# An opening of a two-layer diffusion backbone with its conditioning in four chunks of two feature tiles

## The chip, the cores and the metric

The kernel runs on one core of one Trainium2 chip. The metric is the device time of one execution in microseconds (us). The kernel before takes 2668.5 us, the median of three runs (2668.33 to 2669.18).

## What is computed

A backbone of two layers over 512 latent tokens and 256 context tokens with 1024 features. At the head of each layer stands a conditioned norm: two conditioning vectors (c for the latent tokens, c_ctx for the context) are multiplied with a 1024 x 6144 matrix, and the first two blocks of 1024 columns of the result are the shift and the scale of the first norm. Only layer 0's first norm, its conditioning and the first products behind it bear on this change.

```python
silu_c, silu_cc = jax.nn.silu(c), jax.nn.silu(c_ctx)
for l in range(DEPTH):
    mod_lat = (silu_c @ ada_w[l] + ada_b[l])[:, None, :]
    mod_ctx = silu_cc @ ada_w[l] + ada_b[l]
    sh1, sc1, g1, sh2, sc2, g2 = jnp.split(mod_lat, 6, axis=-1)
    csh1, csc1, cg1, csh2, csc2, cg2 = jnp.split(mod_ctx, 6, axis=-1)
    h_lat = modulate(rmsnorm(x, norm1_g[l]), sh1, sc1)      # h * (1 + scale) + shift
    h_ctx = modulate(rmsnorm(ctx, norm1_g[l]), csh1, csc1)
    z_lat = h_lat @ w_in[l]
    z_ctx = h_ctx @ w_in[l]
    ...
```

Behind it come attention, two other branches and a feed-forward network, which the change leaves as they are. Everything is fp32.

## The kernel before

**Layout.** Activations lie feature-major: eight tiles x of 128 features by 768 tokens (T); `pa` is the part of the 512 latent tokens, `pb` that of the 256 context tokens, and index s (0 latent, 1 context) picks the modulation `mod[0][s]` (in listings mod00 and mod01). The norm's output of tile k is held as two tiles, `hh` (rounded to fp32r, TensorE's fast fp32 format) and `hl` (what the rounding left).

**Products.** A gemm (L164 to L186) takes each product of two fp32 matrices as three of fp32r ones: whi x hh (L183), whi x hl (L184), wlo x hh (L186). `Stream` brings the weights in halves of 512 KB on SP's DMA queue (L62) into two raw buffers; ACT casts whi (L83), and VectorE subtracts wlo (L69). With `late` set, wlo is written where `low()` stands and not at once. The products of silu(c) with the conditioning matrix are plain fp32 ones instead ("whole" here): stationary `silu` (128 x 2), moving 512 columns (L216).

**The opening**, `startup` (L413). SP's queue brings the eight x tiles (384 KB each) with the raw conditioning tiles (512 KB each, `Raw`, L113, seven buffers) between them. The conditioning of shift and scale goes in chunks n of 512 columns, each of four raw tiles: n=2 is the scale of tiles 0 to 3, n=0 their shift; n=3 and n=1 are scale and shift of tiles 4 to 7. `ada_pe` makes a chunk's eight products on TensorE, copies the sum from PSUM (L222, ACT), turns it with four small products against `ident` (L228) and adds the bias (L206). n=2 and n=0 are made this way while x arrives. Beside them `sq_acc` squares each x (ACT, L317 and L323) and sums the squares (VectorE, L324), `norm_stat` brings the sum across features with small products (L335) and takes the inverse root on VectorE, and `norm_rows` spreads it over the partitions (TensorE L349, ACT copy L351, tile rb).

**The norm and the first gemm.** `scales_set` (L308) makes acol = (1 + scale) * g. `norm_apply` (L360) makes for each tile nt = x * acol * rb (VectorE, L367), hh = nt + shift (ACT, L376) and hl = nt + shift - hh (VectorE, L379). The gemm that eats them is that of three weight halves (keys "c"); `step(k, part, i)` issues the three products of tile k, token part and half i. Tiles 0 to 3 come first, latent then context; in between go chunk n=3 on VectorE (`ada_dve`: sixteen multiply-adds of 512 columns, L244 and L246, then small products against `ones`) and chunk n=1 on TensorE, two products at a time. Then follow tiles 4 to 7, and `finish(pb, 4)` issues the context part of tiles 4 to 7 half by half and evacuates each half (`c_first`: ACT copies halves 0 and 2, L792; VectorE multiplies half 1 into the copy of half 0, L794). Then `attn_load` sends two transfers (rl and cs, 256 KB each) from POOL's queue (L594, L596), and the query/key products of layer 0 (L647) begin.

**What sets the order.** Nothing reorders: each engine works through its own list in program order, which the Python code above writes out by hand. A tile of a rotating buffer (`bufs=2`) waits until the last reader of the one before it is done; a DMA on SP's queue that waits for its buffer holds the DMAs behind it.

## Time and profile before

| what | us |
|---|---|
| median of three runs | 2668.5 |
| the profiled execution's own time | 2669.8 |
| its span (first to last instruction) | 2667.9 |
| TensorE busy in the span | 2613.4 (98%) |
| VectorE, ACT, POOL busy | 1630.2, 1035.4, 220.3 |
| mean granted clock of TensorE over the span | 0.995 |

The page of the profile comes from one execution. "Granted clock" is the TensorE clock that the throttle gave, as a share of full speed. A busy TensorE is not one at its peak: its products overlap, and their ends are modelled, so the opening is read by the starts of its products. Times are from the span's start.

### The profile page before, as it was taken

What the parts mean: (1) busy time and instruction counts of PE and PEld (TensorE: products, weight loads), DVE (VectorE), ACT (ScalarE), POOL (GpSimd) and SP (SyncE); (2) the same over time, 40 slices, a digit from 0 to 9 for tenths busy, and PEclk for the clock granted to TensorE, in tenths of its full rate; (3) what the DMA queues carried; (4) which work ended last, traced back from release to release, by engine and by line L of the source; (5) the groups of instructions that cost most, each with busy time, mean ns of one, the idle gap of its engine ahead of it and who ended that gap; (6) DMA issues with size and microseconds to landing.
All of it is one profiled execution on the core that took longest, in us unless ns stands there. A gap on an engine that the chain in (4) does not pass through costs nothing.

```text
span 2667.9 us, 37365 instructions
## 1 busy us (share of the span) xinstructions
PE 2613.4 (98%) x15128; PEld 2265.6 (85%) x15128; DVE 1630.2 (61%) x2887; ACT 1035.4 (39%) x1840; POOL 220.3 (8%) x202
## 2 busy tenths in 40 slices
PE   7999999999999999999999999999999999999999
PEld 3899999888888888888888878898988888888887
DVE  5677777656546537544544577777767554654544
ACT  3455555542122224312312344555563232443422
POOL 0000000001111110100100100000001122010101
PEclk9999999999999999999999999999999999999999
DMA  5211211224333332222222231212124545233233
GB/s 225 82 44 58 63 67 44 65 67 148 105 125 111 103 127 66 78 86 73 79 79 79 91 108 60 68 53 63 56 72 170 174 165 182 72 100 100 93 103 111
DMA packets 79660, 254.36 MB, mean 95 GB/s; under 512 B 9200, under 2 KB 19712, under 8 KB 79104
## 3 DMA queue, kind: packets, MB, share of 16 engines
q1 hardware_dynamic: 64512, 196.64, 22.7%
q0 software_dynamic: 14544, 55.07, 6.3%
q8 instruction: 119, 1.95, 0.3%
q14 instruction: 53, 0.43, 0.0%
q10 hardware_dynamic: 432, 0.27, 0.0%
HBM read 234.63 MB, written 6.82 MB: 91 GB/s over the span
## 4 chain that ended last, share of the span: by engine, by line
PE 82%; DVE 10%; ACT 4%; DMA 2%; issue 1%; SPq 0%; POOL 0%; ACTq 0%; POOLq 0%; DVEq 0%
PE mm L183 22%; PE mm L186 22%; PE mm L184 22%; PE S L857 3%; DVE wlo L69 2%; PE mm L647 2%; PE mm L649 2%; PE mm L648 2%; ACT whi L83 1%; PE mmT L893 1%; DMA qT<-qT 1%; ACT pa L869 1%; DVE zs L697 1%; DVE al L898 1%; PE mmT L906 1%
## 5 line engine op out<-in xcount | busy, mean ns | idle before, releaser
L183 PE MATMUL mm<-hh,whi 128*128 128x512 f32 (+1 forms) x2392 | 853.3, 357 | 7.3 <-ACT hh L376 5.5
L184 PE MATMUL mm<-hl,whi 128*128 128x512 f32 (+1 forms) x2392 | 818.8, 353 | 6.9 <-DVE hl L379 6.5
L186 PE MATMUL mm<-hh,wlo 128*128 128x512 f32 (+1 forms) x2392 | 751.3, 353 | 1.3 <-DVE wlo L69 1.3
L183 PEld LDWEIGHTS mm<-hh,whi 128*128 128x128 f32 x2392 | 451.8, 189 | 99.9 <-ACT hh L376 9.3
L69 DVE TENSOR_TENSOR wlo<-wraw,whi 128x1024 fp32r<-128x1024 f32 x320 | 399.0, 1247 | 196.6 <-ACT whi L83 194.8
L184 PEld LDWEIGHTS mm<-hl,whi 128*128 128x128 f32 x2392 | 452.1, 189 | 72.2 <-DVE hl L379 13.7
L186 PEld LDWEIGHTS mm<-hh,wlo 128*128 128x128 f32 x2392 | 414.0, 190 | 40.7 <-DVE wlo L69 3.0
L83 ACT CAST whi<-wraw 128x1024 fp32r<-128x1024 f32 x320 | 334.9, 1048 | 284.0 <-PE mm L184 243.2
L1018 DVE SCALAR_TENSOR_TENSOR cv<-mm,pc,cv 128x511 f32<-128x511 f32 (+1 forms) x132 | 86.8, 657 | 181.4 <-ACT cv L1017 180.5
L869 ACT ACTIVATE pa<-S,mn 128x768 f32<-128x768 f32 (+1 forms) x160 | 129.3, 813 | 154.7 <-DVE mn L864 127.3
L183 PE MATMUL mm<-ah,whi 128*128 128x512 f32 (+1 forms) x528 | 187.9, 356 | 0.0
L647 PE MATMUL mm<-whi,hh 128*128 128x256 f32 x640 | 183.5, 287 | 1.3 <-DVE cp L794 0.8
L648 PE MATMUL mm<-wlo,hh 128*128 128x256 f32 x640 | 181.1, 283 | 0.0
L649 PE MATMUL mm<-whi,hl 128*128 128x256 f32 x640 | 181.1, 283 | 0.0
L184 PE MATMUL mm<-al,whi 128*128 128x512 f32 (+1 forms) x528 | 179.9, 354 | 0.0
L186 PE MATMUL mm<-ah,wlo 128*128 128x512 f32 (+1 forms) x528 | 161.7, 355 | 0.0
L1017 ACT ACTIVATE cv<-mm,pc 128x512 f32<-128x512 f32 (+1 forms) x132 | 88.7, 705 | 176.9 <-PE mm L186 176.9
L1179 DVE SCALAR_TENSOR_TENSOR x<-mm,mod,x 128x512 f32<-128x512 f32 (+1 forms) x91 | 58.2, 659 | 139.0 <-PE mm L186 139.0
L1222 POOL TENSOR_TENSOR cv<-cv 128x768 f32<-128x768 f32 (+1 forms) x44 | 91.5, 2080 | 601.2 <-DVE cv L1020 419.9
L857 PE MATMUL S<-kT,qT 128*128 128x512 f32 x576 | 119.1, 343 | 11.4 <-DMA qT<-qT 9.7
L647 PEld LDWEIGHTS mm<-whi,hh 128*128 128x128 f32 x640 | 122.5, 191 | 4.3 <-ACT cp L792 1.0
L864 DVE TENSOR_REDUCE mn<-S 128x1 f32<-128x768 f32 x128 | 116.2, 948 | 12.8 <-PE S L857 12.8
(237 smaller groups left out, 4035.2 us busy)
## 6 DMA issues: line engine op xcount, KB each, us to landing
wraw<-w SPq DMA_DIRECT2D x320, 512.0 KB, 3.6
araw<-ada POOLq DMA_DIRECT2D x80, 512.0 KB, 4.0
qT<-qT SPq DMA_DIRECT2D x80, 128.0 KB, 3.9
araw<-ada SPq DMA_DIRECT2D x16, 512.0 KB, 8.7
x<-xT SPq DMA_DIRECT2D x8, 384.0 KB, 7.4
srow<-sscr POOLq DMA_DIRECT2D x3, 1024.0 KB, 6.1
x<-xT POOLq DMA_DIRECT2D x8, 384.0 KB, 6.4
xscr<-x SPq DMA_DIRECT2D x8, 256.0 KB, 4.0
```

The source lines that it names most:

```text
L69: self.lo_eng.tensor_tensor(lo, raw, hi.bitcast(F32), ALU.subtract)
L83: self.nc.scalar.copy(hi, raw)
L183: nc.tensor.matmul(ps[:, :m], lhsT=hh, rhs=xh[:, o:o + m], start=st, stop=False)
L184: nc.tensor.matmul(ps[:, :m], lhsT=hh, rhs=xl[:, o:o + m], start=False, stop=False)
L186: nc.tensor.matmul(ps[:, :m], lhsT=hl, rhs=xh[:, o:o + m], start=False, stop=sp)
L647: nc.tensor.matmul(ps[:, :256], lhsT=hh[:, sl], rhs=hi[:, c:c + 256], start=(k == 0), stop=False)
L648: nc.tensor.matmul(ps[:, :256], lhsT=hh[:, sl], rhs=lo[:, c:c + 256], start=False, stop=False)
L649: nc.tensor.matmul(ps[:, :256], lhsT=hl[:, sl], rhs=hi[:, c:c + 256], start=False, stop=(k == 7))
L857: nc.tensor.matmul(s[:, c0 + o:c0 + o + m], lhsT=st["q"][:, v, a, t0:t0 + 128], rhs=st["k"][a][:, k0 + o:k0 + o + m], start=(v == 0), stop ...
L864: nc.vector.tensor_reduce(mn[:, a:a + 1], ss[a], AX.X, ALU.min)
L869: nc.scalar.activation(pa[:, :nk], ss[a], AF.Exp, bias=mn[:, a:a + 1], scale=-1.0, accum_out=sm[a])
L1222: nc.gpsimd.tensor_tensor(cs[1][:, :n], cs[1][:, :n], cs[0][:, :n], ALU.mult)
```

## The change

`startup` is written anew. The conditioning is cut into four chunks j, each of two feature tiles (2j and 2j+1) with both shift and scale: 256 columns of the one and 256 of the other, in four raw tiles of 512 KB as before. The host packs the matrix so (`layout`).

- Chunks 0 and 1 are whole fp32 products as before (`ada_pe` with `whole`, eight each).
- Chunks 2 and 3 are split: `ada_split` casts a raw tile to ahi on ACT (L213) and subtracts alo (L215) on VectorE for the even pieces, on POOL for the odd ones; ahi and alo have two buffers each. The stationary side, `silu4`, has four columns (hi and lo of the two vectors), and TensorE makes 16 fp32r products of 512 moving columns for each such chunk (L229). `sel4` adds hi and lo in the four small products that turn a chunk's sum (L240).
- `ada_dve` is gone. The raw conditioning tiles have five buffers and not seven. The squares of an x tile are taken over its 768 columns at once.
- `norm_apply` makes the tiles in pairs, since each pair waits for its chunk's scale (`cut`). rb and the context's nt lie in other buffers. `finish(pb, 6)` is left with two tiles for each half, and the steps of the three halves, the pieces of the chunks and the pairs of tiles are interleaved in a new written order.

Line numbers of the changed kernel: nt L354, hh L363, hl L366, statistics L322, row spread L336, chunk's products L229, its copy L236, its small products L240.

The core of the diff. Functions that are new or written anew stand in full, every line marked +; their old text stands above:

```diff
+    def ada_split(self, l, j, i):
+        nc = self.nc
+        raw = self.ast.take("s", l, j, i)
+        hi = self.ast.pool.tile([128, 1024], F32R, tag="ahi", bufs=2, name="ahi")
+        nc.scalar.copy(hi, raw)
+        lo = self.ast.pool.tile([128, 1024], F32R, tag="alo", bufs=2, name="alo")
+        (nc.vector, nc.gpsimd)[i % 2].tensor_tensor(lo, raw, hi.bitcast(F32), ALU.subtract)
+        self.ast.load_to(len(self.ast.keys) + self.ast.bufs)
+        self.parted.append((hi, lo))
...
+    def ada_pe(self, l, j, ps, whole):
+        nc = self.nc
+        nr = 2 if whole else 4
+        for i in range(4):
+            if whole:
+                parts = [self.ast.take("s", l, j, i)]
+            else:
+                parts = self.parted.pop(0)
+            for q in (0, 1):
+                for p, w in enumerate(parts):
+                    nc.tensor.matmul(ps[0:nr, :], lhsT=(self.silu if whole else self.silu4)[:, 2 * i + q, :],
+                                     rhs=w[:, q * 512:q * 512 + 512], start=(i == q == p == 0),
+                                     stop=(i == 3 and q == 1 and p == len(parts) - 1))
+            if whole:
+                self.ast.load_to(len(self.ast.keys) + self.ast.bufs)
+            yield
+        rows = self.small.tile([4, 512], F32, tag="adarow", bufs=1, name="adarow")
+        nc.scalar.copy(rows[0:nr], ps[0:nr, :])
+        yield
+        pt = self.ad.tile([128, 512], F32, tag="ad", name="ad")
+        for i in range(4):
+            nc.tensor.matmul(pt[:, 2 * i:2 * i + 2], lhsT=rows[0:nr, i * 128:(i + 1) * 128], rhs=self.sel4[0:nr, :],
+                             start=True, stop=True)
+        pv = pt[:, 0:8].rearrange("p (t k s) -> p s t k", t=2, s=2)
+        cut = lambda a: a.rearrange("p (t k) -> p t k", t=2)[:, :, 2 * j:2 * j + 2]
+        for s in range(2):
+            nc.vector.tensor_tensor(cut(self.mod[l][s][:, 0:16]), pv[:, s], cut(self.pc[l][:, PC_ADAB:PC_ADAB + 16]), ALU.add)
...
-    def norm_apply(self, tmp, sc, xs, rb, seg, cut=8, pre=False):
+    def norm_apply(self, tmp, sc, xs, rb, seg, cut=(8,), pre=False):
...
-            t1 = scaled(k + 1) if k + 1 not in (cut, 8) else None
+            t1 = scaled(k + 1) if k + 1 not in cut else None
...
+    def startup(self, xp, xt, load_x, pkeys, evac):
+        nc = self.nc
+        pa, pb = self.parts()
+        self.ast.start(xp, 4, 5, nc.sync)
+        for k in range(8):
+            load_x()
+            if k in (1, 3):
+                self.ast.load_to(self.ast.loaded + 1)
+        self.ws.late = True
+        self.ws.load_to(1)
+        self.ast.load_to(self.ast.bufs)
+        self.parted = []
+        self.silu4 = xp.tile([128, 8, 4], F32R, tag="silu4", bufs=1, name="silu4")
+        nc.scalar.copy(self.silu4[:, :, 0:2], self.silu)
+        nc.vector.tensor_tensor(self.silu4[:, :, 2:4], self.silu, self.silu4[:, :, 0:2].bitcast(F32), ALU.subtract)
+        rb = self.slots.tile([128, T], F32, tag="A0", name="rb")
+        tmp = lambda: xp.tile([128, T], F32, tag="nsq", bufs=2, name="nt")
+        tg = iter(("A1", "A2") * 4)
+        tmpc = lambda: self.slots.tile([128, T], F32, tag=next(tg), name="nt")
+        sc = self.scales(0, 0)
+        self.norm_h()
+        step, finish = self.halves(pkeys, self.segs, evac)
+        cut = (2, 4, 6, 8)
+        ga = self.norm_apply(tmp, sc, [x[:, 0:512] for x in xt], rb[:, 0:512], pa, cut, True)
+        gb = self.norm_apply(tmpc, sc, [x[:, 512:768] for x in xt], rb[:, 512:768], pb, cut)
+
+        def cond(j):
+            ps = (self.mm if j == 1 else self.ad).tile([128, 512], F32, tag="mm" if j == 1 else "ad", name="ad")
+            yield from self.ada_pe(0, j, ps, j < 2)
+            self.scales_set(sc, 0, 0, 2 * j, 2 * j + 2)
+
+        def steps(ks, part, *halves):
+            for i in halves:
+                for k in ks:
+                    step(k, part, i)
+
+        c = [cond(j) for j in range(4)]
+        end = lambda j: next(c[j], None)
+        for i in range(4):
+            next(c[0])
+            if i == 0:
+                self.ast.load_to(8)
+            if i == 2:
+                self.ws.load_to(2)
+            for k in (2 * i, 2 * i + 1):
+                self.sq_acc(xp, k, xt[k], 0, T)
+        next(c[0])
+        r = self.norm_stat(0, T)
+        self.ws.split_to(1)
+        next(c[1])
+        end(0)
+        self.ws.load_to(3)
+        self.ws.low()
+        next(c[1])
+        self.norm_rows(rb[:, 0:512], r, 512)
+        self.norm_rows(rb[:, 512:768], r[:, 4:6], 256)
+        next(ga)
+        next(c[1])
+        next(ga)
+        next(c[1])
+        self.ws.split_to(2)
+        next(c[1])
+        next(ga)
+        self.ws.low()
+        steps((0, 1), pa, 0)
+        end(1)
+        next(ga)
+        steps((0, 1), pa, 1)
+        next(gb)
+        self.ada_split(0, 2, 0)
+        next(ga)
+        self.ada_split(0, 2, 1)
+        next(gb)
+        steps((2,), pa, 0, 1)
+        steps((0, 1), pb, 0, 1)
+        steps((3,), pa, 0, 1)
+        self.ws.split_to(3)
+        next(c[2])
+        self.ada_split(0, 2, 2)
+        next(gb)
+        self.ws.low()
+        next(c[2])
+        self.ada_split(0, 2, 3)
+        next(gb)
+        steps((0, 1, 2), pa, 2)
+        next(c[2])
+        self.ada_split(0, 3, 0)
+        steps((2, 3), pb, 0, 1)
+        next(c[2])
+        next(c[2])
+        self.ada_split(0, 3, 1)
+        steps((3,), pa, 2)
+        steps((0, 1), pb, 2)
+        end(2)
+        next(ga)
+        next(c[3])
+        self.ada_split(0, 3, 2)
+        steps((2, 3), pb, 2)
+        next(ga)
+        next(c[3])
+        self.ada_split(0, 3, 3)
+        steps((4,), pa, 0, 1, 2)
+        next(gb)
+        next(c[3])
+        next(gb)
+        steps((5,), pa, 0, 1, 2)
+        next(c[3])
+        next(c[3])
+        steps((4,), pb, 0, 1, 2)
+        end(3)
+        next(ga)
+        steps((5,), pb, 0, 1, 2)
+        next(ga)
+        steps((6,), pa, 0, 1, 2)
+        next(gb)
+        steps((7,), pa, 0, 1, 2)
+        next(gb)
+        self.ws.low()
+        self.ws.late = False
+        finish(pb, 6)
...
+            self.sel4 = const.tile([4, 2], F32, name="sel4")
+            nc.vector.tensor_tensor(self.sel4, self.ident[0:4, 0:2], self.ident[0:4, 2:4], ALU.add)
...
-            ad[i] = ktile(w[q * 256:(q + 1) * 256])
+        if kind == "s":
+            v = x["ada_w"][l][q * 256:(q + 1) * 256]
+            ad[i] = ktile(np.concatenate([v[:, n * 256:(n + 1) * 256], v[:, D + n * 256:D + (n + 1) * 256]], 1))
```

**TensorE, from its first instruction to the first gemm product** (L183, half 0 of tile 0). ad sums a chunk, st is the statistics and the row spread. Before:

```order
L216 MATMUL ad<-araw,silu 2x512 x10
L228 MATMUL ad<-ident,adarow 128x2 x4
L216 MATMUL ad<-araw,silu 2x512 x3
L335 MATMUL st<-ones,nacc 128x1 x6
L216 MATMUL ad<-araw,silu 2x512 x3
L349 MATMUL st<-ident,rsy 128x128 x4
L228 MATMUL ad<-ident,adarow 128x2 x4
L349 MATMUL st<-ident,rsy 128x128 x2
L183 MATMUL mm<-hh,whi 128x512
```

And in the changed kernel:

```order
L229 MATMUL ad<-araw,silu 2x512 x8
L322 MATMUL st<-ones,nacc 128x1 x6
L229 MATMUL ad<-araw,silu 2x512 x2
L240 MATMUL ad<-sel_83,adarow 128x2 x4
L229 MATMUL ad<-araw,silu 2x512 x2
L336 MATMUL st<-ident,rsy 128x128 x6
L229 MATMUL ad<-araw,silu 2x512 x4
L183 MATMUL mm<-hh,whi 128x512
```

The statistics stood behind thirteen whole products and now stand behind eight; the second eight are all still ahead of the first gemm product.

**ACT, at the first tiles of the norm.** Numbers tell tiles apart. Before, hh_273, 275, 277 and 279 are tiles 0 to 3 (with mod00 the latent part, with mod01 the context's), and whi_324 is the third half:

```order
L376 ACTIVATE hh_273<-nt_289,mod00_87 128x512
L376 ACTIVATE hh_275<-nt_303,mod00_87 128x512
L83 CAST whi_324<-wraw_258 128x1024
L376 ACTIVATE hh_277<-nt_312,mod00_87 128x512
L376 ACTIVATE hh_279<-nt_328,mod00_87 128x512
L376 ACTIVATE hh_273<-nt_360,mod01_88 128x256
L376 ACTIVATE hh_275<-nt_363,mod01_88 128x256
```

In the changed kernel hh_141, 143, 145 and 147 are tiles 0 to 3, whi_360 is the third half, and ahi_318, 326 and 368 are the first three pieces of chunk 2:

```order
L236 COPY adarow_276<-ad_228 2x512
L363 ACTIVATE hh_143<-nt_266,mod00_89 128x512
L363 ACTIVATE hh_145<-nt_297,mod00_89 128x512
L363 ACTIVATE hh_141<-nt_312,mod01_90 128x256
L213 CAST ahi_318<-araw_191 128x1024
L363 ACTIVATE hh_147<-nt_300,mod00_89 128x512
L213 CAST ahi_326<-araw_231 128x1024
L363 ACTIVATE hh_143<-nt_315,mod01_90 128x256
L83 CAST whi_360<-wraw_243 128x1024
L213 CAST ahi_368<-araw_247 128x1024
```

The copy of chunk 1's sums now stands ahead of tile 1's hh, and two casts and tile 3's hh between the context's tiles 0 and 1.

**VectorE, from tile 3's hl to the third half's wlo.** Before (hl_280 is tile 3, wlo_325 the third half, aacc the chunk on VectorE, nt_360 the context's tile 0):

```order
L379 SCALAR_TENSOR_TENSOR hl_280<-nt_328,mod00_87,hh_279 128x512
L69 TENSOR_TENSOR wlo_325<-wraw_258,whi_324 128x1024
L244 TENSOR_SCALAR aacc_349<-araw_240,silu_70 128x512
L244 TENSOR_SCALAR aacc_350<-araw_240,silu_70 128x512
L246 SCALAR_TENSOR_TENSOR aacc_349<-araw_240,silu_70,aacc_349 128x512
L246 SCALAR_TENSOR_TENSOR aacc_350<-araw_240,silu_70,aacc_350 128x512
L367 SCALAR_TENSOR_TENSOR nt_360<-x_109,acol_270,rb_135 128x256
```

In the changed kernel (hl_142, 144, 146 and 148 are tiles 0 to 3; nt_315, 374 and 377 the context's tiles 1 to 3; alo_320 and alo_370 the first and third piece of chunk 2; wlo_361 the third half):

```order
L354 SCALAR_TENSOR_TENSOR nt_315<-x_113,acol_140,rb_138 128x256
L366 SCALAR_TENSOR_TENSOR hl_142<-nt_312,mod01_90,hh_141 128x256
L215 TENSOR_TENSOR alo_320<-araw_191,ahi_318 128x1024
L366 SCALAR_TENSOR_TENSOR hl_148<-nt_300,mod00_89,hh_147 128x512
L366 SCALAR_TENSOR_TENSOR hl_144<-nt_315,mod01_90,hh_143 128x256
L215 TENSOR_TENSOR alo_370<-araw_247,ahi_368 128x1024
L354 SCALAR_TENSOR_TENSOR nt_374<-x_117,acol_140,rb_138 128x256
L354 SCALAR_TENSOR_TENSOR nt_377<-x_119,acol_140,rb_138 128x256
L366 SCALAR_TENSOR_TENSOR hl_146<-nt_374,mod01_90,hh_145 128x256
L69 TENSOR_TENSOR wlo_361<-wraw_243,whi_360 128x1024
L366 SCALAR_TENSOR_TENSOR hl_148<-nt_377,mod01_90,hh_147 128x256
```

The third half's wlo stood ahead of the context's first nt and now stands behind its last. On POOL the four odd pieces' subtractions stand ahead of the two transfers of `attn_load`, which came first there before.

## Rows read from the trace of the kernel before

**Rows 1.** Timeline of TensorE: start, duration (us), operation, count [idle before, its releaser].
```profile
32.08 0.50 PE L183 MATMUL mm<-hh,whi 128*128 128x512 f32 x1 [1.08 <-ACT hh L376]
...
75.98 0.28 PE L184 MATMUL mm<-hl,whi 128*128 128x256 f32 x1
76.10 0.28 PE L186 MATMUL mm<-hh,wlo 128*128 128x256 f32 x1
...
77.19 0.36 PE L647 MATMUL mm<-whi,hh 128*128 128x256 f32 x1 [0.81 <-DVE cp L794]
```

**Rows 2.** Timeline of TensorE: whole products of a later chunk, then split ones.
```profile
49.31 1.88 PE L216 MATMUL ad<-araw,silu 128*2 128x512 f32 x4
...
69.64 0.39 PE L186 MATMUL mm<-hh,wlo 128*128 128x512 f32 x1
69.87 0.39 PE L183 MATMUL mm<-hh,whi 128*128 128x512 f32 x1
```

**Rows 3.** Waits of TensorE, 30 to 77.3 us: total us, times, longest.
```profile
PE mm L183 <- ACT hh L376: 2.5, 3, 1.1
PE mm L184 <- DVE hl L379: 2.1, 3, 1.5
```

**Rows 4.** Windows: PE, PEld, DVE, ACT, POOL busy; granted clock, DMA share, GB/s.
```profile
32.00:34.00 2.00, 1.46 (x4) 0.67 (x4) 1.94 (x3) 0.63 (x2) 0.00 (x0) 0.99 1.04 416
34.00:36.00 2.00, 0.68 (x2) 0.58 (x3) 1.97 (x3) 0.00 (x0) 0.00 (x0) 0.50 1.01 403
...
44.00:46.00 2.00, 2.00 (x7) 0.79 (x6) 1.78 (x5) 1.33 (x3) 0.00 (x0) 0.95 0.78 154
```

**Rows 5.** Timeline of TensorE and ACT: last raw wait, last Square, statistics.
```profile
17.59 1.88 PE L216 MATMUL ad<-araw,silu 128*2 128x512 f32 x4 [0.67 <-DMA araw<-ada]
...
22.09 0.94 ACT L323 ACTIVATE nsq<-x 128x512 f32<-128x512 f32 x2 [0.45 <-DVE nacc L324]
...
24.03 1.50 PE L335 MATMUL st<-ones,nacc 128*128 128x1 f32 x12
```

**Rows 6.** Timeline of TensorE: small products of tiles 4 to 7, first products.
```profile
60.54 0.41 PE L228 MATMUL ad<-ident,adarow 2*128 2x2 f32 x4
...
62.88 0.50 PE L183 MATMUL mm<-hh,whi 128*128 128x512 f32 x1 [0.35 <-ACT hh L376]
63.66 0.50 PE L184 MATMUL mm<-hl,whi 128*128 128x512 f32 x1 [0.29 <-DVE hl L379]
```

**Rows 7.** Groups by form, 0 to 80 us: busy us, mean ns | idle before.
```profile
L69 DVE TENSOR_TENSOR wlo<-wraw,whi 128x1024 fp32r<-128x1024 f32 x5 | 6.1, 1220 | 3.5 <-ACT whi L83 3.5
...
L379 DVE SCALAR_TENSOR_TENSOR hl<-nt,mod,hh 128x256 fp32r<-128x256 f32 x8 | 3.9, 481 | 0.5 <-ACT hh L376 0.5
...
L376 ACT ACTIVATE hh<-nt,mod 128x512 fp32r<-128x512 f32 x8 | 5.5, 720 | 4.1 <-DVE nt L367 4.1
...
L83 ACT CAST whi<-wraw 128x1024 fp32r<-128x1024 f32 x5 | 5.2, 1047 | 7.1 <-DMA wraw<-w 7.1
...
L222 ACT COPY adarow<-ad 2x512 f32<-2x512 f32 x3 | 1.7, 576 | 15.0 <-PE ad L216 15.0
```

**Rows 8.** Timeline of ACT: the copies of half 0's context and of others.
```profile
73.54 0.37 ACT L792 COPY cp<-mm 128x256 f32<-128x256 f32 x1 [2.23 <-PE mm L186]
...
75.87 0.92 ACT L792 COPY cp<-mm 128x512 f32<-128x512 f32 x2
```

**Rows 9.** Timelines of POOL and VectorE near 623 us; one group by form.
```profile
623.28 2.17 POOL L1149 TENSOR_TENSOR mp<-mp,sg 128x768 f32<-128x768 f32 x1 [4.37 <-ACT whi L83]
...
623.05 0.69 DVE L274 SCALAR_TENSOR_TENSOR junk<-araw,srow 128x512 f32<-128x512 f32 x1
623.78 2.22 DVE L274 SCALAR_TENSOR_TENSOR junk<-araw,srow 128x512 f32<-128x512 f32 x1
...
L1170 POOL TENSOR_TENSOR sg<-sg,mp 128x768 f32<-128x768 f32 x8 | 14.7, 1841 | 73.7 <-DVE sg L1169 73.7
```

**Rows 10.** Windows: one of 5 us.
```profile
1774.00:1779.00 5.00, 4.63 (x23) 4.43 (x24) 2.12 (x3) 2.67 (x5) 0.00 (x0) 0.66 0.31 107
```

More of the change, by code (lines that the diff above doesn't have):

```diff
@@ L471, in startup @@
-        step(3, pa, 1)
-        two(g3)
-        two(g1)
-        for k in range(4):
-            next(gb)
-            for i in range(3):
-                step(k, pb, i)
-            if k:
-                two(g3)
-                if k == 3:
-                    for _ in g3:
-                        pass
-                two(g1)
-        step(0, pa, 2)
-        step(1, pa, 2)
-        for _ in g1:
-            pass
-        step(2, pa, 2)
-        step(3, pa, 2)
-        self.scales_set(sc, 0, 0, 4, 8)
@@ L491, in startup @@
-        next(ga)
-        for k in range(4, 8):
-            step(k, pa, 0)
-            step(k, pa, 1)
-            next(ga if k < 7 else gb)
-        for k in range(4, 8):
-            if k < 7:
-                next(gb)
-            step(k, pa, 2)
+            for k in (2 * i, 2 * i + 1):
[6 more added lines that the diff above has]
+        self.ws.load_to(3)
+        self.ws.low()
@@ L500, in startup @@
+        steps((6,), pa, 0, 1, 2)
+        next(gb)
+        steps((7,), pa, 0, 1, 2)
+        next(gb)
         self.ws.low()
         self.ws.late = False
-        finish(pb, 4)
+        finish(pb, 6)
     def parts(self):
```

93 lines of the change are left out of this document (removed).

## The prediction

> **What bounds the kernel now.** I read the timeline of each engine, the waits, the windows, and the orders of both programs. The change ends at the first query/key product of layer 0, which starts at 77.19 us [rows 1]; behind it the two programs list the same work on every engine, so the whole change is the shift of that product. TensorE has its first gemm product at 32.08 and its last of the opening at 76.10 [rows 1]. What lies in these 45.1 us is counted from spacings: a 512-column split product takes 0.23 us and a 256-column one 0.12 (differences of starts), two whole fp32 products 1.88 [rows 1, 2]. 72 of the first and 72 of the second make 25.2 us, the four pairs of chunk 1 7.5, the small products and the sums of the VectorE chunk some 2 (an estimate): 34.7 us. The other 10.4 are waits, of which the row names 2.5 us for hh, 2.1 for hl [rows 3] and 0.8 for the last evacuation [rows 1], and the clock: TensorE was granted half speed from about 34.0 to 44.2 [rows 4], 10.2 us, of which up to half is lost (5.1). It fell when TensorE had waited again and again for the first hh and hl, no more than 1.1 us at a time up to there.
>
> **Up to the first product: no gain.** The change needs one chunk for tiles 0 and 1, but the PE order above shows all eight whole products of chunk 1 still ahead of the first gemm product, and the statistics ahead of all eight. The statistics need the last x tile. Before, the fifth raw tile of the SP queue was awaited until 17.59 [rows 5]; up to it stood 5 x 512 + 5 x 384 KB, with 512 KB of the POOL queue (rl, cs) beside them: 4992 KB. Now x7 has 4 x 512 + 8 x 384 = 5120 KB up to it, and rl and cs stand behind POOL's four subtractions. 128 KB more, at the 0.4 MB/us of [rows 4], is 0.3 us: x7 is there at about 17.9. From the Square of the last x to the first statistics product it takes 22.09 to 24.03, 1.9 us [rows 5]: 19.8. Then, in order on TensorE: statistics 1.5 [rows 5], eight whole products 4 x 1.88 = 7.5, four small products 0.4 [rows 6], the broadcast of six 128-column whole products at a quarter of 0.94 each, 1.4: 30.6. TensorE has nothing to do from the end of chunk 0 (about 15, an estimate) to 19.8, far longer than any wait just ahead of 34.0, so I let it begin at half clock and lose 0.6 to 1.7: first product at 31.2 to 32.3, against 32.08. I take 31.5.
>
> **From there, what TensorE must do.** The same gemm, 25.2, and 32 split products with 4 stationary and 512 moving columns. The trace has none of these; the bounds are 0.12 (256 columns) and 0.94 (a whole fp32 one), I take 0.23 as for the other split ones of 512 columns: 7.4. Three groups of small products, 1.2. Sum 33.8, 1 us less than before. The sixteen VectorE multiply-adds of the old chunk go; TensorE waited for none of them but the sums, so I price them at nothing.
>
> **What it will wait for.** I walk the ACT and VectorE orders with the durations of [rows 7].
> - Tile 1. Its hh stands on ACT behind the copy of chunk 1's sums, which waits for TensorE's last whole product. Copy 0.58, hh 0.72, hl and its handover 0.78 [rows 6], 2.2 with the first handover; TensorE has four products, 0.9: wait 1.3.
> - Tiles 2, 4 and 6 each begin a new chunk: small products, mod, scale, nt, hh, hl. Before, this chain took from 60.54 to 62.88, and hl's product came 0.78 later [rows 6]. Between, TensorE has 0.4 and six 512-column products (1.4), or some 256-column ones (1.1): 0.5 to 0.8 for hh and 0.55 for hl. With other work ahead of it in VectorE's queue I take 1.3, 1.6 and 1.6.
> - Context half of tile 1. On ACT two casts (ahi, 1.05 each) and hh of tile 3 (0.72) stand ahead of its hh (0.48, as the VectorE step of that size): 3.3 us behind the hh of context tile 0. TensorE then has only three 256-column products, done 0.8 behind it: wait 2.4. Its hl is later still if POOL holds VectorE (below): 2.3 more.
> - Third weight. VectorE's order has alo of the third piece, two nt and an hl ahead of wlo. That piece's cast needs a buffer (there are two) that is free only when TensorE has used the first piece. From there: cast 1.05, alo 1.22, nt, hh and hl 0.48 each, wlo 1.22 = 4.9; TensorE has four split products and two of the third half, 1.4: wait 3.6.
> - The fourth chunk's second piece: 0.6 (an estimate; its cast stands behind an hh).
> - The end. The next products need the evacuations of all three halves. Before, ACT copied the context of half 0 at 73.54 [rows 8], 2.6 ahead of TensorE's last product, and had time for two casts. Now each half has two tiles left at the end, 0.72 us, not four: half 0 is done 1.4 ahead, and copy 0.37 [rows 8], casts 2.1, two more copies 0.9 and handovers make 3.8: 2.4 behind the last product, where it was 1.1.
> These are 1.3 + 4.5 + 4.7 + 3.6 + 0.6 + 2.4 = 17.1 us.
>
> **POOL beside VectorE.** Two of each later chunk's four subtractions go to POOL. A 128x1024 one is not in the trace; 768 elements take 1.84 [rows 9], so 2.45 by size; the bounds are 1.84 and the disturbed 2.17 scaled, 2.9. What it does to VectorE is in [rows 9]: the POOL product from 623.28 to 625.45 leaves a VectorE operation of 0.69 us at 2.22, done just behind POOL's end. So the hl of context tile 1 (two SBUF operands, like that one) is held from the second cast's end, 2.8 behind the hh of context tile 0, for 2.45, and its product comes 2.3 later than that of its hh. If it is not held, these 2.3 us go. The other three I price at nothing where VectorE has slack, and let rival 3 hold them.
>
> **Clock.** Context tile 1 and the third weight each make TensorE wait over 3 us within a few; it fell before on less [rows 4]. A short low stretch of this trace lies at 1774: in those 5 us the mean granted clock is 0.66 [rows 10], so half speed for 0.34 x 5 / 0.5 = 3.4 us, 1.7 lost. Two of them: 3.4; bounds 0 and, with two more, 6.8.
>
> **Sum.** 31.5 + 33.8 + 17.1 + 3.4 = 85.8 against 77.19: 8.6 us slower. The profiled execution took 2669.8 us, the runs' median is 1.3 below it; 2668.5 + 8.6 = 2677.1. On SP the last raw tiles and the fourth weight come later, behind buffers that the splits free, but nothing above waits for them; rl and cs go out when POOL is done and are first read behind the query/key products of head 0: free.
>
> **Rivals.**
> 1. POOL does not hold VectorE: 2.3 off, and with less waiting one low stretch less, 1.7: +4.6, 2673.1. For: the two engines meet only if the casts fall so. Against: [rows 9].
> 2. The clock holds through the waits: +5.2, 2673.7. For: waits of 1 us and more at 63 left it alone [rows 6]. Against: [rows 4].
> 3. All four POOL subtractions hold VectorE, and a second one of them is on the path (in front of the scale of tile 4): 2.4 more, and one low stretch more, 1.7: +12.7, 2681.2. For: the casts set POOL off just as VectorE gets its hh. The Trainium skill (SBUF — State Buffer, Who interferes with whom) says that a VectorE instruction with two SBUF inputs and a GpSimd instruction that reads SBUF shut each other out for the whole instruction, whichever began first; by it every one of the four blocks. The trace agrees for the pair it shows (2.22 for 0.69).
> 4. Not slower: the splits are ahead of use, as their place in the order says. ACT's queue is the point: if ahi is cast while TensorE still has chunk 1, the waits at context tile 1, the third weight and chunk 3 (8.9) and the clock that they cost (3.4) are gone: 8.6 - 12.3 = -3.7, 2664.8; 1 us less with the first products at high clock. It decides at one row: wlo of the third weight done before TensorE's second piece of chunk 2. Against it: two buffers, and casts that stand behind hh.
>
> **How the numbers follow.** A measurement of this kernel tells 0.2%, 5.3 us, from no change. Forecast 0.50, slower by more than that; rivals 1 and 2 0.14 each, just under that bound, so half each; rival 3 0.12, slower; rival 4 0.10, 0.06 of it beyond 0.2%. Slower 0.50 + 0.14 + 0.12 = 0.76, the same 0.14 + 0.04 = 0.18, faster 0.06. The range takes in rivals 1 to 3 and the bounds: no hold and no low stretch, 8.6 - 2.3 - 3.4 = +2.9; four low stretches, +12.0; with some 1.5 us below and 1 above for the estimates, 2670 to 2682.
>
> **What would show it.** In the profile after: first gemm product at 31 to 33; the query/key product near 86; TensorE waiting 2 us and more for the hh of context tile 1, then for an hl that begins when POOL ends, 3 to 4 us for wlo of the third weight; VectorE operations of 2 us beside POOL's; granted clock at half in two stretches between 40 and 60. A first product at 25, or no wait over 1.5 us from 37 to 60, would make this wrong.

## The result, and the profile after

The changed kernel takes 2682.47 us, the median of six runs (2680.38 to 2683.89), against 2668.41 of the kernel before (six runs): a ratio of 1.0057, with a 95% interval of 1.0046 to 1.0067. It is 14.1 us slower. The forecast was slower by 8.6 us, 2677.1, with a range up to 2682.0: the right direction, and a time just outside the range.

The profiled execution took 2680.38 us, its span is 2678.6. The timeline of TensorE in the changed kernel (start, duration in us, operation, count [idle before, its releaser]):

```profile
13.48 1.88 PE L229 MATMUL ad<-araw,silu 128*2 128x512 f32 x4 [0.74 <-DMA araw<-ada]
19.75 2.72 PE L322 MATMUL st<-ones,nacc 128*128 128x1 f32 x12 [4.40 <-DVE nacc L311]
...
33.96 0.50 PE L183 MATMUL mm<-hh,whi 128*128 128x512 f32 x1
...
36.83 1.05 PE L240 MATMUL ad<-sel,adarow 2*128 2x2 f32 x8
37.80 0.51 PE L183 MATMUL mm<-hh,whi 128*128 128x512 f32 x1
...
42.34 0.28 PE L186 MATMUL mm<-hh,wlo 128*128 128x256 f32 x1
44.50 0.38 PE L183 MATMUL mm<-hh,whi 128*128 128x256 f32 x1 [1.88 <-ACT hh L363]
46.94 0.58 PE L184 MATMUL mm<-hl,whi 128*128 128x256 f32 x1 [2.06 <-DVE hl L366]
...
51.10 0.39 PE L229 MATMUL ad<-alo,silu 128*4 128x512 f32 x1
51.33 0.39 PE L229 MATMUL ad<-ahi,silu 128*4 128x512 f32 x1
...
52.95 0.39 PE L184 MATMUL mm<-hl,whi 128*128 128x512 f32 x1
56.70 0.50 PE L186 MATMUL mm<-hh,wlo 128*128 128x512 f32 x1 [3.36 <-DVE wlo L69]
...
88.33 0.28 PE L186 MATMUL mm<-hh,wlo 128*128 128x256 f32 x1
90.86 0.35 PE L664 MATMUL mm<-whi,hh 128*128 128x256 f32 x1 [2.25 <-DVE cp L811]
```

The first gemm product comes at 33.96, 1.9 us later than before, and the first query/key product at 90.86, 13.7 later [rows 1]. Between them lie 56.9 us, where before there were 45.1. The waits stand where the prediction looked for them: the hh and then the hl of the context's tile 1 (44.50 and 46.94), wlo of the third half (56.70), the evacuations (90.86). The sums of TensorE's waits from 30 to 91 us (total us, times, longest) have grown against [rows 3]; the line for wlo is new, and the last one was a single 0.81 [rows 1]:

```profile
PE mm L183 <- ACT hh L363: 4.0, 5, 1.9
PE mm L186 <- DVE wlo L69: 3.4, 1, 3.4
PE mm L184 <- DVE hl L366: 3.2, 5, 2.1
PE mm L664 <- DVE cp L811: 2.2, 1, 2.2
```

The clock, in windows of 2 us (columns as in [rows 4]; the granted clock is the number behind POOL's):

```profile
18.00:20.00 2.00, 0.25 (x2) 0.25 (x2) 1.59 (x2) 1.89 (x3) 0.00 (x0) 0.89 1.02 408
20.00:22.00 2.00, 2.00 (x11) 2.00 (x11) 0.00 (x0) 0.00 (x0) 0.00 (x0) 0.50 1.03 412
...
26.00:28.00 2.00, 2.00 (x11) 1.29 (x12) 0.80 (x5) 0.00 (x0) 0.00 (x0) 0.91 0.47 164
46.00:48.00 2.00, 1.06 (x5) 1.06 (x6) 0.89 (x1) 0.00 (x0) 0.60 (x1) 0.71 0.42 160
...
56.00:58.00 2.00, 1.30 (x4) 1.07 (x5) 2.00 (x2) 0.34 (x1) 1.99 (x1) 0.77 0.51 174
...
80.00:82.00 2.00, 1.71 (x5) 1.11 (x6) 2.00 (x4) 0.78 (x2) 0.00 (x0) 0.75 0.00 0
```

Half speed was granted from about 19.6 to 26.4, while TensorE worked without a break behind its wait of 4.4 us, and then in three stretches of 3.4 us, from 46.8, 57.1 and 81.0 on, each behind a wait or a pair of them. A fourth of that length, from 91.2 on and behind the wait of 2.25, lies behind the query/key product and so outside the 56.9.

POOL beside VectorE, the four POOL subtractions and the VectorE operations that lie beside them:

```profile
44.12 2.49 POOL L215 TENSOR_TENSOR alo<-araw,ahi 128x1024 fp32r<-128x1024 f32 x1 [36.97 <-ACT ahi L213]
56.01 2.87 POOL L215 TENSOR_TENSOR alo<-araw,ahi 128x1024 fp32r<-128x1024 f32 x1 [9.41 <-ACT ahi L213]
65.08 2.38 POOL L215 TENSOR_TENSOR alo<-araw,ahi 128x1024 fp32r<-128x1024 f32 x1 [6.20 <-ACT ahi L213]
71.60 2.54 POOL L215 TENSOR_TENSOR alo<-araw,ahi 128x1024 fp32r<-128x1024 f32 x1 [4.14 <-ACT ahi L213]
```

```profile
44.48 2.41 DVE L366 SCALAR_TENSOR_TENSOR hl<-nt,mod,hh 128x256 fp32r<-128x256 f32 x1
...
56.56 2.60 DVE L366 SCALAR_TENSOR_TENSOR hl<-nt,mod,hh 128x256 fp32r<-128x256 f32 x1
...
65.88 0.23 DVE L245 TENSOR_TENSOR mod<-ad,pc 128x4 f32<-128x4 f32 x2 [2.65 <-PE ad L240]
66.08 1.48 DVE L295 SCALAR_TENSOR_TENSOR acol<-mod,pc 128x2 f32<-128x2 f32 x2
...
71.80 2.62 DVE L354 SCALAR_TENSOR_TENSOR nt<-x,acol,rb 128x256 f32<-128x256 f32 x1
```

Each of the four holds VectorE to its own end, which the held operation passes by 0.1 to 0.3 us: the first is the hl of the context's tile 1, of 0.48 us as a rule [rows 7] and of 2.41 here, and the hl of the same size at 56.56 took 2.60. The third is the plainest: two adds with one operand in PSUM (L245) ran in 0.23 us in the middle of POOL's subtraction, and the two operations behind them, of 2 elements each but with both tensors in SBUF (L295), ended at 67.56, just behind POOL's 67.46.

What lies behind the opening did not change: from the first query/key product to the end of the span are 2590.7 us before, 2587.7 after, and 2587.5 to 2591.4 in every kernel below. Most of that spread is the clock again: summed over windows of 20 us from 100 to 2640, (1 - granted clock) x 20 comes to 8.8 us before and 5.2 after, and to 5.2 and 8.6 in the kernels with 2587.5 and 2591.4 (e6_best and e7_best_pool). So I go by the start of that product and by the stretch from the first gemm product to it, beside the times.

### The profile page after: what moved, and what is told of

It is laid out like the page before. It is cut to its first block, busy times and chain, and to the rows that moved or that the text cites. A ratio compares the mean times of both kernels' runs of the same rounds, so it can differ in the third digit from the quotient of the medians.

```text
span 2678.6 us, 37412 instructions
## 1 busy us (share of the span) xinstructions
PE 2617.6 (98%) x15148; PEld 2270.5 (85%) x15148; DVE 1632.1 (61%) x2874; ACT 1041.4 (39%) x1842; POOL 230.5 (9%) x206
## 4 chain that ended last, share of the span: by engine, by line
PE 82%; DVE 10%; ACT 4%; issue 1%; DMA 1%; SPq 0%; POOL 0%; ACTq 0%; POOLq 0%; DVEq 0%
PE mm L183 22%; PE mm L186 22%; PE mm L184 22%; PE S L874 3%; PE mm L664 2%; PE mm L666 2%; PE mm L665 2%; DVE wlo L69 2%; PE mmT L910 1%; ACT whi L83 1%; DMA qT<-qT 1%; ACT pa L886 1%; DVE al L915 1%; DVE zs L714 1%; PE mmT L923 1%
## 5 line engine op out<-in xcount | busy, mean ns | idle before, releaser
L183 PE MATMUL mm<-hh,whi 128*128 128x512 f32 (+1 forms) x2392 | 853.9, 357 | 8.7 <-ACT hh L363 6.9
L183 PEld LDWEIGHTS mm<-hh,whi 128*128 128x128 f32 x2392 | 451.8, 189 | 99.4 <-ACT hh L363 10.7
L183 PE MATMUL mm<-ah,whi 128*128 128x512 f32 (+1 forms) x528 | 187.9, 356 | 0.0
L665 PEld LDWEIGHTS mm<-wlo,hh 128*128 128x128 f32 x640 | 122.8, 192 | 0.1
```

The costliest lines, as they stand in the source:

```text
L183: nc.tensor.matmul(ps[:, :m], lhsT=hh, rhs=xh[:, o:o + m], start=st, stop=False)
L665: nc.tensor.matmul(ps[:, :256], lhsT=hh[:, sl], rhs=lo[:, c:c + 256], start=False, stop=False)
```

## The experiments

The first column of times is the median of the kernel's runs, whose times spread by 2.6 us (e8_warm5) to 8.8 (e4_order); "first" and "qk" are the starts of the first gemm product and the first query/key product in its profiled execution, which is one of these runs and can lie some 3 us from the median. The kernel before was run again beside each group: 2668.9 beside e1 to e4, 2668.2 beside e5 to e8, 2667.6 beside e9 to e12.

| kernel | us | ratio to before, interval | first | qk | between |
|---|---|---|---|---|---|
| before | 2667.6 to 2668.9 | | 32.08 | 77.19 | 45.1 |
| changed | 2682.47 | 1.0046 to 1.0067 | 33.96 | 90.86 | 56.9 |
| e1_dve | 2683.79 | 1.0040 to 1.0070 | 35.79 | 89.21 | 53.4 |
| e2_whole | 2680.67 | 1.0031 to 1.0061 | 35.56 | 87.49 | 51.9 |
| e3_warm | 2680.28 | 1.0028 to 1.0062 | 32.41 | 89.28 | 56.9 |
| e4_order | 2674.47 | 1.0013 to 1.0034 | 36.27 | 85.78 | 49.5 |
| e5_order_dve | 2674.87 | 1.0014 to 1.0032 | 35.17 | 80.84 | 45.7 |
| e6_best | 2659.04 | 0.9951 to 0.9976 | 29.60 | 67.09 | 37.5 |
| e7_best_pool | 2664.40 | 0.9978 to 0.9996 | 31.69 | 72.75 | 41.1 |
| e8_warm5 | 2677.45 | 1.0021 to 1.0048 | 30.23 | 86.98 | 56.8 |
| e9_warm5_dve | 2674.70 | 1.0016 to 1.0037 | 30.14 | 82.07 | 51.9 |
| e10_best_whole | 2667.31 | 0.9989 to 1.0008 | 31.02 | 76.32 | 45.3 |
| e11_best_nofill | 2661.64 | 0.9970 to 0.9988 | 33.02 | 70.46 | 37.4 |
| e12_warm5_order | 2670.89 | 1.0002 to 1.0020 | 30.12 | 79.25 | 49.1 |

**e1_dve: three POOL subtractions on VectorE.**

```diff
-        (nc.vector, nc.gpsimd)[i % 2].tensor_tensor(lo, raw, hi.bitcast(F32), ALU.subtract)
+        (nc.gpsimd if (j, i) == (3, 3) else nc.vector).tensor_tensor(lo, raw, hi.bitcast(F32), ALU.subtract)
```

> Three of the four POOL subtractions (alo) go to VectorE; the last one stays on POOL, so that the transfers of rl and cs go out as late as in the changed kernel. In the changed kernel the first query/key product starts at 90.86 us and the hl of the context's tile 1 makes TensorE wait 2.06. Theory A (a POOL subtraction holds VectorE's two-operand work): alo takes 1.23 on VectorE where the hold took up to 2.5, so that wait shrinks to about 1, no VectorE operation of 2 us and more is left before 70, one low stretch of the clock goes with it, and the first query/key product starts at 87 to 89. Rival B (POOL is harmless and VectorE is the engine that is short): VectorE gets 3 x 1.23 us more ahead of the same hl and wlo, and the product starts at 91 to 94. In both, the wait for the third half's wlo stays at 3 us and more.

The hl's wait went from 2.06 to 1.10, the low stretches between from three to two, and the stretch is 3.5 us shorter: theory A, in the trace. The product itself, at 89.21, missed the expected 87 to 89, because in this execution the start came out longer, in which nothing was edited. The time did not fall either; its trace fits that, but only e9_warm5_dve tests it. The clock at the start:

```profile
16.00:20.00 4.00, 0.72 (x4) 0.72 (x4) 2.89 (x4) 3.21 (x5) 0.00 (x0) 0.63 1.03 411
20.00:28.00 8.00, 8.00 (x23) 4.12 (x24) 2.70 (x18) 0.00 (x0) 0.00 (x0) 0.50 0.86 315
28.00:30.00 2.00, 2.00 (x4) 0.25 (x2) 0.91 (x1) 0.00 (x0) 0.00 (x0) 0.50 0.36 96
30.00:32.00 2.00, 2.00 (x12) 1.27 (x12) 0.00 (x0) 0.07 (x1) 0.00 (x0) 0.83 0.71 254
```

Half speed lasted 0.37 x 4 / 0.5 + 10 + 0.17 x 2 / 0.5 = 13.6 us here, the first 2.2 of it still within the wait of 4.5, against 6.8 in the changed kernel's execution. From the start of the statistics to the first gemm product it took 16.5 us here, 14.2 in the changed kernel, 16.7 and 15.9 in e4_order and e5_order_dve, which have the same start. So this start differs between executions by up to 2.5 us, and the median of the changed kernel, 2.1 above its profiled execution, would fit longer ones.

**e2_whole: chunks 2 and 3 whole too.**

```diff
-            yield from self.ada_pe(0, j, ps, j < 2)
+            yield from self.ada_pe(0, j, ps, True)
...
-        self.ada_split(0, 2, 0)
```

(and the seven other splits; nine raw buffers.)

> Chunks 2 and 3 as whole fp32 products too; no ahi, no alo, raw buffers nine in place of five and the freed ahi/alo. TensorE has 16 products at 0.94 us in place of 32 at 0.23: 7.7 us more. Theory A (casts and subtractions stand in the way on ACT and VectorE): the waits of 1.88 and 2.06 at the context's tile 1 shrink to under 1 together, the wait of 3.36 for wlo goes, and the three low stretches from 46 to 85 (1.7 each) go; the opening up to the statistics gets up to 1.3 later since rl and cs go out early again; the first query/key product starts at 84 to 88 although TensorE works more. Rival C (the pairs' chains of copy, small products, scale, nt, hh, hl cost the time, the splits do not): the product starts at 98.

87.49: within 84 to 88, though the start was slow (35.56). With 7.7 us more of products the stretch is 5.0 us shorter, no wait for a wlo is left, no hh or hl is awaited for over 0.72, and the clock is full in it. Rival C falls. In the changed order, the splits cost more than they save, by 5.0 us in the stretch. The time shows 1.8 of it: rl and cs go out at 6.2 us again, TensorE waits 3.63 for a raw tile, and the statistics begin 1.5 later, at 21.29.

**e3_warm and e8_warm5: TensorE kept at work ahead of the statistics.**

```diff
+        pw = self.mm.tile([128, 512], F32, tag="mm", name="mw")
+        for i in range(5):
+            nc.tensor.matmul(pw[0:2, :], lhsT=self.silu[:, i % 8, :], rhs=xt[0][:, 0:512], start=True, stop=True)
         r = self.norm_stat(0, T)
```

(eight in e3_warm, five in e8_warm5.)

> Eight whole products of an x tile into a PSUM bank that nobody reads, between chunk 0 and the statistics, where TensorE waits 4.4 us for the last square. Theory D (the first gemm product comes at 33.96 and not at 31.5 because TensorE had the half clock from about 19.5 to 26.3): the clock stays full, the statistics products take 1.5 and not 2.72, and the first gemm product starts at 30.7 to 31.5; the first query/key product starts 2 to 3 us earlier than 90.86. Rival E (the first gemm product is bound by the chain of statistics, root, row spread, nt and hh, not by TensorE's clock): it starts at 33 or later.

The clock held, but the first gemm product came at 32.41, between the two theories. The reason was the experiment's: the last sum of squares was done at 18.92, and the eight products went on to 21.3.

```profile
14.37 7.03 PE L449 MATMUL mw<-x,silu 128*2 128x512 f32 x16
21.33 1.50 PE L322 MATMUL st<-ones,nacc 128*128 128x1 f32 x12
```

> e3_warm with five products in the gap in place of eight: eight took 7.03 us (14.37 to 21.33) and so ended over 2 us behind the last sum of squares (18.92), which is why the first gemm product came at 32.41 and not at 30.7 to 31.5. Theory D: five end at about 18.8, the clock stays full, and the first gemm product starts at 29.8 to 30.8, the first query/key product at 86 to 88. Rival E (the chain behind the statistics bounds the first gemm product): 32 or later again.

30.23 and 86.98: theory D. Of the 3.7 us at the first gemm product 0.6 are an earlier start of the statistics (19.15), 3.1 the clock. The statistics and what follows run at full clock,

```profile
14.00:20.00 6.00, 5.86 (x20) 1.70 (x18) 3.83 (x4) 4.79 (x6) 0.00 (x0) 1.00 1.03 409
20.00:26.00 6.00, 6.00 (x29) 2.86 (x30) 3.61 (x18) 0.00 (x0) 0.00 (x0) 1.00 1.02 408
```

and five products whose result nobody reads make the kernel 5.0 us faster (2677.45). The stretch behind stays at 56.8. These 5.0 us are more than the 3.9 by which the product comes earlier in the profile, as they would be if most runs of the changed kernel had a longer low stretch than its profiled one.

**e4_order: order alone.**

```diff
         next(gb)
-        self.ada_split(0, 2, 0)
         next(ga)
-        self.ada_split(0, 2, 1)
         next(gb)
+        self.ws.split_to(3)
+        self.ws.low()
+        self.ada_split(0, 2, 0)
+        self.ada_split(0, 2, 1)
         steps((2,), pa, 0, 1)
...
         steps((3,), pa, 0, 1)
-        self.ws.split_to(3)
         next(c[2])
         self.ada_split(0, 2, 2)
         next(gb)
-        self.ws.low()
```

> Order alone: the first two pieces of chunk 2 are split behind the hh of the context's tile 1, and cast and subtraction of the third half stand ahead of them. Nothing is added or taken away. Theory F (where the splits stand in ACT's and VectorE's order costs the time): the waits of 1.88 and 2.06 at the context's tile 1 go down to 0.3 each, the wait of 3.36 for wlo goes, the low stretches at 46.8 and 57.1 go with them (1.7 each); chunk 2's first split product waits 1 to 2 us for alo instead; the first query/key product starts at 81 to 84. Rival B (ACT and VectorE are short as such): the waits only move to chunk 2's products, and it starts at 88 or later.

The waits at the context's tile 1 and for wlo are gone (0.40 for one hl is left), 1.02 for POOL's alo and 1.37 for a later hl have come:

```profile
50.48 0.40 PE L229 MATMUL ad<-alo,silu 128*4 128x512 f32 x1 [1.02 <-POOL alo L215]
...
56.19 0.38 PE L184 MATMUL mm<-hl,whi 128*128 128x256 f32 x1 [1.37 <-DVE hl L366]
```

The stretch from first to qk is 7.4 us shorter. One low stretch of the clock is left in it, from 75.8 on, where there were three; the two that went, at 1.7 us lost each, make 3.4 of the 7.4. The product came at 85.78 and not at 81 to 84 since this execution too had the long low stretch at its start. The time is 8.0 us down: theory F, and the largest single part.

**e5_order_dve: that order, alo on VectorE.**

> The order of e4_order, and three of the four POOL subtractions on VectorE as in e1_dve (the last stays on POOL). In e4_order TensorE needs 49.5 us from its first gemm product (36.27) to the first query/key product (85.78); the waits of 1.02 for POOL's alo and of 1.37 for an hl stand in it. Theory A (POOL's subtraction is slow and holds VectorE): both go or shrink to under 1.2 together, and the stretch takes 46 to 47.5 us. Rival B (VectorE is short): 49 us or more. When the first gemm product comes (34 to 36.5) depends on how long the half clock lasts behind the 4.4 us wait, which this kernel leaves alone.

45.7 us, a little under the 46 to 47.5 expected: the wait for alo is gone and that for the hl shrank to 0.86, theory A in the trace. Of the 3.8 us against e4_order 1.7 are the low stretch at 75.8, behind tile 6's waits, which is missing here. That stretch stands in the trace of every kernel with the changed conditioning and POOL's four subtractions (changed, e3, e4, e8, e12) and in none with one (e1, e5, e9), though tile 6's waits are the same, 0.72 and 0.29. The time, 2674.87, is that of e4_order; what POOL costs in that order could not be told from the times.

**e9_warm5_dve and e12_warm5_order: e8_warm5 with one part each.** The edits are those of e1_dve and e4_order.

> e8_warm5 (the start's clock held) with three of the four POOL subtractions on VectorE as in e1_dve: the share of POOL in the changed kernel without the luck of the start's low stretch, which was 6.8 us in one profiled execution and 13.7 in the others. e8_warm5 takes 2677.45 us, 56.75 from its first gemm product (30.23) to the first query/key product (86.98). Theory A (POOL's hold is on the path at the context's tile 1): the hl's wait falls from 2.06 to 1.1 and one or two of three low stretches go, the stretch takes 53 to 54.5 us and the kernel 2674 to 2676. Rival G (POOL's hold is hidden in the changed order, since the waits for casts and for wlo behind it take up what is saved): 55.5 us or more, and 2676.5 to 2678.5.

2674.70, and 51.9, under the 53 to 54.5 expected: 2.75 us less than e8_warm5, and one low stretch in place of three before the product. Theory A; this is POOL's share where the start's clock does not blur it. Most of it is clock: the hl's wait fell by 1.0 us and hh's by 0.6, two low stretches fewer give 3.4. The eight times, 2671.75 to 2678.86, overlap those of e8_warm5 (2676.37 to 2678.96), so the share is rough.

> e8_warm5 with the order of e4_order: POOL keeps its four subtractions. Theory (the order's 8.0 us and the start's clock, 5.0 us, are two separate losses): 2682.5 - 8.0 - 5.0 = 2669.5, so 2668 to 2671, and the first query/key product at 78 to 81. Rival K (the order gained by its low stretches alone, which the held clock takes away): 2673 to 2677.

2670.89, and the product at 79.25, both as expected: the start's clock and the order add up, 5.0 + 6.6 us, and with both the kernel is still no faster than before.

**e6_best: the causes taken away together.** The main places, as added lines; what they replace is shown for the first alone (alo is on VectorE throughout; rl's transfer waits for tile 0's hh):

```diff
-            if k in (1, 3):
+            if k in (1, 3, 5):
...
+        pw = self.mm.tile([128, 512], F32, tag="mm", name="mw")
+        for i in range(4):
+            nc.tensor.matmul(pw[0:2, :], lhsT=self.silu[:, i % 8, :], rhs=xt[0][:, 0:512], start=True, stop=True)
+        next(c[1])
         r = self.norm_stat(0, T)
...
+        self.ws.split_to(2)
+        self.ws.low()
         self.norm_rows(rb[:, 0:512], r, 512)
...
+        next(ga)
         next(c[1])
+        next(gb)
+        next(gb)
+        steps((0,), pa, 0)
+        end(1)
+        next(ga)
+        steps((0,), pa, 1)
+        steps((1,), pa, 0, 1)
+        steps((0, 1), pb, 0, 1)
+        self.ada_split(0, 2, 0)
...
+        steps((6,), pa, 0)
+        steps((7,), pa, 0)
+        steps((6,), pa, 1)
+        steps((7,), pa, 1)
+        finish(pb, 6, lambda: steps((6, 7), pa, 2))
```

> The changed kernel's chunks and splits with the causes found so far taken away: all alo on VectorE; the splits, the second and third half's wlo and the context's tiles at places of the order where ACT and VectorE are free; the last two tiles' latent part of half 2 behind halves 0 and 1, so that their copies and the next casts lie beside products; one raw tile of chunk 1 loaded ahead of x6, its two products and four products that nobody reads between chunk 0 and the statistics; rl's transfer behind tile 0's hh on POOL's queue. Theory (order, POOL and clock are what the changed kernel lost): first gemm product at 29.5 to 31, no low stretch of the clock before the first query/key product, waits between of some 4 us in all, so 25.2 + 7.4 + 2 + 4 = 38.6 us from one to the other: the query/key product at 68 to 70, against 77.19 in the kernel before, and 6 to 9 us less than the kernel before in all. Rival B (ACT and VectorE cannot carry casts and subtractions beside the norm): waits of 8 us and more in that stretch, the product at 75 or later, and no gain over the kernel before that can be told.

It takes 2659.04 us: 9 us less than the kernel before (interval 0.49 to 0.24%) and 23 less than the changed one. The first query/key product, at 67.09, comes even before the 68 to 70 expected. The waits of TensorE from 30 us to it are one line,

```profile
PE mm L675 <- DVE cp L822: 0.9, 1, 0.9
```

and in the profiled execution (2656.45, the shortest of the five) the clock is full throughout:

```profile
14.00:30.00 16.00, 15.81 (x61) 6.07 (x60) 11.46 (x28) 8.32 (x12) 1.21 (x3) 1.00 1.00 382
30.00:67.00 37.00, 36.22 (x200) 27.25 (x198) 28.85 (x53) 21.58 (x32) 0.08 (x1) 1.00 0.34 115
```

From the first gemm product to the query/key product are 37.5 us, with 35.5 of work. Rival B falls: ACT and VectorE carry the casts and subtractions beside the norm. Between e12_warm5_order and this kernel lie 11.9 us; POOL and the splits are taken apart below, the other moves (the context's tiles, the end, chunk 1's raw tile) were not tried one by one.

**e7_best_pool, e10_best_whole, e11_best_nofill: e6_best with one part put back.**

> e6_best with the odd pieces' subtractions on POOL, as the changed kernel has them. Theory A (a POOL subtraction holds VectorE's operations on two SBUF operands as long as it runs, 2.5 us for work that VectorE does in 1.23): VectorE operations of over 2 us beside each of POOL's four, and the first query/key product 3 to 6 us later than in e6_best. Rival B (two engines share the subtractions, VectorE gains 4 x 1.23 us): it starts at the same time or earlier.

5.4 us slower in time, and 3.6 in the stretch; these 3.6 are what the trace puts down to POOL. The product came 5.7 later, but 2.1 of that is the start, in which nothing was edited: behind a wait of 0.56 for the statistics, half clock came for 3.4 us all the same.

```profile
22.00:24.00 2.00, 2.00 (x12) 1.48 (x12) 1.45 (x10) 0.00 (x0) 0.00 (x0) 0.72 1.02 408
24.00:26.00 2.00, 2.00 (x4) 0.25 (x2) 1.90 (x9) 0.86 (x1) 0.00 (x0) 0.50 1.03 412
26.00:28.00 2.00, 2.00 (x14) 1.37 (x12) 1.40 (x2) 0.35 (x2) 0.00 (x0) 0.93 0.62 236
```

Two of POOL's four, and VectorE's operations beside them (an hl of 0.48, a scale of 2 elements in a group of two); beside the other two an nt of 0.48 us is held in the same way:

```profile
43.91 2.67 POOL L215 TENSOR_TENSOR alo<-araw,ahi 128x1024 fp32r<-128x1024 f32 x1 [3.19 <-ACT ahi L213]
50.69 2.41 POOL L215 TENSOR_TENSOR alo<-araw,ahi 128x1024 fp32r<-128x1024 f32 x1 [4.11 <-ACT ahi L213]
```

```profile
44.25 2.62 DVE L366 SCALAR_TENSOR_TENSOR hl<-nt,mod,hh 128x256 fp32r<-128x256 f32 x1
...
51.00 2.18 DVE L295 SCALAR_TENSOR_TENSOR acol<-mod,pc 128x2 f32<-128x2 f32 x2
```

> e6_best with chunks 2 and 3 as whole fp32 products, no ahi and alo, nothing else moved (nine raw buffers). Theory H (a split chunk is worth the 3.8 us of TensorE that it saves, once its casts and subtractions are out of the way): 16 products at 0.88 to 0.94 for 32 at 0.23 are 6.7 to 7.7 us more on a TensorE that waits for nothing, so the first query/key product comes at 74 to 75 against 67.09, and the time is 2665 to 2667. Rival I (splitting pays nothing, the order alone does): under 69, and 2661 or less.

2667.31, 8.3 us slower, no better than the kernel before, and 7.8 of it in the stretch: theory H, though both figures lie above its ranges: the time by 0.3, the product, at 76.32, by 1.3, since here too the start had a low stretch and came 1.4 later. Splitting two chunks is worth what it takes off TensorE, 7.8 us, but only once nothing waits for it.

> e6_best without the four products that nobody reads ahead of the statistics. Theory D (the wait ahead of the statistics costs clock behind it): TensorE waits 3 to 3.5 us in pieces between chunk 0's end and the statistics, the clock falls for 3.4 us or more, the first gemm product comes at 30.5 to 33 against 29.60, and the time is 1 to 4 us longer. Rival J (the two real products of chunk 1 in the gap are enough): the same time within 1 us.

2.6 us slower, the first gemm product at 33.02, the stretch behind unchanged. TensorE waited 1.62 and 2.08 us in the gap and was then at half clock for 6.8 us: theory D again. The gain in time is less than the 3.4 us between the two profiled starts; e7_best_pool and e10_best_whole show that the filled start can lose some clock too.

## Why the prediction was wrong, step by step

The sum was 31.5 + 33.8 + 17.1 + 3.4 = 85.8. In the changed kernel it is 33.96 for the first product, 25.2 + 7.4 + 2.9 = 35.5 of work, three low stretches of 1.7 = 5.1, and 16.3 of waits for the rest: 90.86. So the walk along the orders held, and three terms were too small: the first product by 2.5, which is the clock of the start, the small products by 1.7, the clock between by 1.7.

- **First product, 31.5: failed, by 2.5.** The statistics began at 19.75 (forecast 19.8), by two small misses that cancel: the last Square began at 17.62 (17.9), the statistics 2.1 behind it (1.9). "Far longer than any wait just ahead of 34.0, so I let it begin at half clock and lose 0.6 to 1.7" was the step: half speed came, but for 6.8 us, some 3.1 lost, and in the executions of e5_order_dve and e1_dve, with the same start, for 10.2 and 13.6. The trace of before had shown a low stretch of 10.2 us [rows 4] as well as one of 3.4 [rows 10]; pricing the start by the short one had no ground. e8_warm5 confirms it: without the low stretch the first product comes at 30.23, and the time is 5.0 us less.
- **Work, 33.8: 1.7 too low.** A split product of 4 stationary columns takes 0.23 as taken (51.10 to 51.33). The three groups of small products were priced by the old transposes, 0.41 [rows 6]; against `sel4` they are fp32 products, which the row counts twice each (x8 for four), and take 0.98 (36.83 to 37.80).
- **Waits, 17.1: right to 0.6 us or less at each place.** From the starts in the timeline, less the product ahead: tile 1, 1.2 (1.3 forecast); tiles 2, 4 and 6, 1.1 + 1.3 + 1.4 (4.5); the context's tile 1, 2.0 + 2.3 (4.7); the third half's wlo, 3.5 (3.6); the end, 2.4 (2.4). The fourth chunk's second piece cost nothing (0.6). These are 15.3 of the 16.3; the other 1.0 lies in gaps of some 0.1 us. e4_order shows that they were the order's, as walked.
- **POOL: the mechanism right.** 2.38 to 2.87 us for a subtraction (2.45 taken, bounds 1.84 and 2.9). All four held VectorE, as rival 3 said. The Trainium skill (SBUF — State Buffer, Who interferes with whom) states that a VectorE instruction with two SBUF inputs contends with a GpSimd one that reads SBUF, and that one with at most one SBUF input, outside the two-port modes, does not. The trace agrees with both: the four operations above have two SBUF inputs, and the adds with a PSUM operand (L245) ran in 0.23 us. Of rival 3's price the 2.4 were not there: the scale of tile 4 was held for 1.3 us, but chunk 3's products covered it, and TensorE waited there for no more than at tile 6. Its one low stretch more did come.
- **Clock between, 3.4: one stretch too few**, the one at 81.0 behind tile 6's waits of 0.72 and 0.29. Where three of POOL's four went to VectorE (e1, e5, e9) these waits are just as long and the stretch is missing, so POOL has a part in it that the runs do not explain.
- **Rivals 1, 2 and 4** did not come about. Rival 4's mechanism is real all the same: with the splits truly ahead of use, e6_best is 9 us faster than before, not the 3.7 worked out there; in it the start's clock, POOL's hold and part of the end's wait went too. With the order and the start's clock alone (e12_warm5_order) nothing was gained over the kernel before. Rival 2's "waits of 1 us and more at 63" are two of 0.35 and 0.29 in [rows 6], some 1.1 us together by the starts, so they were weaker evidence than they read.
- **Profiled execution and median.** The former rose by 10.6 us, the median by 14.1. The product came 13.7 later in the profile; behind it the kernel before had 3.0 us more in its profiled execution (2590.7 against 2587.7). That longer low stretches at the start put the other runs of the changed kernel above its profiled one is likely, but those runs left no trace. Their mean granted clocks fit: 0.993 in the three slowest, 0.994 in the three others.

Why e5_order_dve's times do not show the 3.8 us that its profiled stretch gained over e4_order is answered in part: neither execution is typical. That of e4_order took 2.9 us more than its median, that of e5_order_dve, the shortest of its ten, 2.5 less. So the two traces overstate the gain; how much of it is real stays open.

## What to carry to other kernels

Work moved off the bound engine pays only if the engines that take it over have it behind them when it is asked for: a kernel with the same split chunks was 14 us slower in one order and, with POOL left out and the start filled, 9 faster in another. Read the order of every engine that feeds the bound one, and put first what is awaited first. A wait of the bound engine ahead of a long dense stretch should be priced with the clock behind it, and filled, be it with products that nobody reads; where the fill left half a us open (e7_best_pool, e10_best_whole), 3.4 us of half clock came all the same.
